# The order of small matmuls over the partition groups, and second factors on 128 partitions, in a two-layer RWKV-7 and mLSTM trunk

## The chip, the cores and the metric

The kernel runs on one core of one Trainium2 chip. The metric is the device time of one execution in microseconds (us), from the median of several runs. A core has TensorE (PE in the profile; its weight loads are listed apart as PEld), VectorE (DVE), ScalarE (ACT), GpSimd (POOL) and SyncE (SP), which issues most of the DMAs. The granted clock of TensorE stands in the profile as a share: 1.00 is 2.4 GHz and 0.50 is 1.2 GHz.

## What is computed

The input is a sequence of 1024 frames of 1024 features, and all is fp32. Layer 0 mixes time with RWKV-7, layer 1 with a chunkwise mLSTM, each is followed by a SwiGLU block, and a norm ends it. What the change touches is the following.

```python
w_log = -softplus(-(w0 + tanh(wl) @ w2)) - 0.5          # decay: second factor w2, 64 x 1024
a = sigmoid(a0 + al @ a2)                               # rate: second factor a2, 64 x 1024

def _rwkv7_step(state, inp):                            # per head, 64 x 64 state, frame by frame
    r_t, w_t, k_t, v_t, a_t, b_t = inp
    sa = einsum('bhvk,bhk->bhv', state, a_t)
    state = state * w_t[:, :, None, :] + sa[..., None] * b_t[:, :, None, :] + v_t[..., None] * k_t[:, :, None, :]
    return state, einsum('bhvk,bhk->bhv', state, r_t)

# mLSTM, in chunks: the scores of queries and keys, times a decay mask
w_intra = exp(d_log - m_t[..., None]) * einsum('bhctd,bhcsd->bhcts', q, k)
```

There are 16 RWKV heads of 64 features and 8 mLSTM heads with 64 features for queries and keys.

## The kernel before

The RWKV recurrence is computed in chunks of 64 frames. A chunk needs the inverse of a unit triangular 64 x 64 matrix, which is built from small blocks. The work is cut into 16 tasks: 8 pairs of heads (128 partitions are two heads of 64) by two halves of 512 frames, so that a task holds 8 chunks of two heads each. The method `chunks` runs the tasks as a pipeline. In step i it calls `rw_chain` for task i-3 (the recurrence over the 8 chunks), `rw_solve` for task i-2, `rw_inverse` for task i-1, `rw_prep` for task i and `rw_finish` for task i-3. Between these calls it takes pieces from a list of fillers: the large projections of the second half (values, decay, rate, keys, receptances, gate) and later the output projection. The fillers are matmuls of 128 x 128 weights on 512 columns, of type fp32r.

A scheduling layer puts each engine's instructions into their final order ahead of time, from the program's order, from priorities (`ahead`) and from what it takes to be ready. On the chip each engine then runs its list in that order and waits on semaphores.

PSUM has eight banks under these tags: `dn` twice, and `c1`, `c2`, `px`, `iv`, `sc`, `tr` once each. The profile leaves numbers out of names, so `c1` and `c2` are both `c` there. A tag with one bank is free for its next user when the reader of the last has read it.

An fp32 matmul appears in the trace as two records, each with a weight load; an fp32r matmul is one record. A shape such as `64*128` in a row counts the partitions that the weights span, and the output partitions. A matmul with weights on 64, 32 or 16 partitions uses one part of the array, its tile; the partitions of the operands and of the output set which.

`rw_inverse` (L657): VectorE inverts 16 x 16 diagonal blocks (L675, L677); a trip through DRAM puts them on four partition groups, q = 0 to 3, at partitions 32q. Two products join them to 32 x 32 blocks: 32 matmuls into `iv` (L701), a copy by ScalarE, and 32 more (L709). Then, for e = 0 and e = 1 one after the other (e is the parity of the chunk), two products of 8 matmuls each join these to 64 x 64 (L724 and L728), with a copy by ScalarE behind each (L725 and L729) and a bank `iv` for each. The index c counts the 8 blocks of a parity.

`rw_solve` (L731): values and one operand are transposed; then 16 matmuls into `px` (L758), copied to `Z`, and 16 more into `px` (L765), copied to `VU` by two ScalarE instructions (L767 and L768). Last, for e = 0 and then 1, eight matmuls go into `tr` (L775) and VectorE copies them into `AR` (L776). `rows(c)` gives the partition halves that chunk c uses.

`ml_prep` (L1284): for the two heads h of a pair, four matmuls of 64 x 128 weights on 128 columns make the scores (L1325) in a bank that alternates between `sc` and `iv`, and VectorE multiplies them by the mask (L1326). It runs eight times.

`lora` (L428): decay and rate, for each half of the frames. The first factor's columns stand twice, so that its output has 128 rows in two equal halves. `st` holds the rounded weights (high part) on rows 0 to 63 and the rest (low part) on rows 64 to 127; `th` and `tl` are high and low part of the activations. L448 is one matmul of `st` on `th`, and L449 one of `hi` on `tl`, on 64 partitions. There are 8 column blocks in each of four calls, so 32 such pairs.

Every matmul that `mm` issues has the line L207 in the profile, so tiles tell them apart.

## Time and profile before

| | |
|---|---|
| median of 3 runs | 3062.93 us (3058.17 to 3084.75) |
| profiled execution | 3071.16 us |
| its span | 3069.2 us |
| mean granted clock of TensorE | 0.919 |
| TensorE busy | 2875.5 us, 94% of the span |
| VectorE, ScalarE busy | 2041.1 us, 1409.5 us |
| the pipeline of RWKV tasks | about 220 to 1180 us of the span |
| the mLSTM mixer | about 1840 to 2360 us of the span |

A span is the profiled part of one execution. Matmuls are pipelined: the time of a record holds its way through the array, and what a matmul costs in a stream is the distance from its start to the next one's start. In the rows of the timeline, equal instructions that follow each other are one row, with the start of the first, the time from there to the end of the last, and their count behind the x.

### The profile page before, as it was taken

Reading aid. Unit: us, or ns where it says so; the run is one execution under the profiler, and the core shown is the slowest. Engines: PE = TensorE matmul, PEld = TensorE weight load, DVE = VectorE, ACT = ScalarE, POOL = GpSimd, SP = SyncE. Lnnn points to the kernel's source line nnn. Section 1 sums busy time; section 2 is a strip of 40 time slices with the busy share of each in tenths; the row PEclk is TensorE's granted clock in tenths of the full one; section 3 lists DMA queues with packets and bytes.
Section 4 is the critical chain, followed back from the end, with each engine's and each line's share of the span. In section 5 each row is a group of like instructions: output and inputs, shape, how many; then the busy total and the mean of one; then the engine's idle time right before and its main releaser. Section 6 shows DMA issues by size and latency. Waiting matters only on the chain.

```text
span 3069.2 us, 46769 instructions
## 1 busy us (share of the span) xinstructions
PE 2875.5 (94%) x17080; PEld 2254.1 (73%) x17080; DVE 2041.1 (67%) x4029; ACT 1409.5 (46%) x2641; POOL 73.5 (2%) x98
## 2 busy tenths in 40 slices
PE   6799989999989898999999998999989999999998
PEld 5577657677767677788877776777857788887776
DVE  7866665757666545978887758755555766667645
ACT  5756665656655554532224335322344533332532
POOL 0000000000000000000000000000010000000000
PEclk9899767979979689999999999988989999999999
DMA  8774433435354236466778854344545233336734
GB/s 289 258 236 141 111 98 92 116 101 142 102 155 125 80 95 210 151 191 220 239 243 281 270 178 157 115 124 151 158 134 168 93 117 103 103 114 229 256 120 149
DMA packets 359721, 492.38 MB, mean 160 GB/s; under 512 B 125212, under 2 KB 208796, under 8 KB 359492
## 3 DMA queue, kind: packets, MB, share of 16 engines
q1 hardware_dynamic: 345668, 464.24, 47.9%
q10 hardware_dynamic: 13824, 25.17, 2.2%
q8 instruction: 134, 2.20, 0.3%
q14 instruction: 95, 0.78, 0.1%
HBM read 359.77 MB, written 129.50 MB: 159 GB/s over the span
## 4 chain that ended last, share of the span: by engine, by line
PE 61%; DVE 13%; DMA 12%; issue 7%; ACT 5%; POOL 1%; SPq 1%; DVEq 0%; POOLq 0%; ACTq 0%
PE dn L207 23%; PE c L207 18%; PE iv L207 8%; PE px L207 6%; PE sc L207 4%; DMA tt<-gd 2%; DMA wraw<-in_wdn 2%; DMA wraw<-wsd 1%; DMA bgs<-in_ada 1%; DVE wq L212 1%; ACT wq L211 1%; DVE ga L212 1%; PE tr L207 1%; DMA bgs<-in_wdn 1%; DMA wsd<-bgs 1%
## 5 line engine op out<-in xcount | busy, mean ns | idle before, releaser
L207 PE MATMUL dn<-a,whi 128*128 128x512 f32 (+1 forms) x1224 | 473.2, 451 | 19.1 <-ACT a L211 7.8
L207 PE MATMUL c<-ga,wq 128*128 128x512 f32 x1446 | 355.6, 395 | 10.2 <-ACT ga L211 8.6
L211 ACT ACTIVATE wq<-wraw 128x1024 fp32r<-128x1024 f32 x202 | 210.7, 1057 | 330.9 <-DVE wraw L890 82.0
L207 PEld LDWEIGHTS c<-ga,wq 128*128 128x128 f32 x1446 | 271.9, 190 | 76.2 <-ACT ga L211 11.5
L207 PEld LDWEIGHTS dn<-a,whi 128*128 128x128 f32 (+1 forms) x1224 | 242.8, 206 | 89.4 <-issue 14.6
L212 DVE TENSOR_TENSOR wq<-wraw,wq 128x1024 fp32r<-128x1024 f32 x202 | 244.3, 1221 | 85.1 <-ACT wq L211 84.8
L207 PE MATMUL dn<-a,wlo 128*128 128x512 f32 (+2 forms) x640 | 284.1, 448 | 7.6 <-ACT tmp L420 3.0
L207 PE MATMUL c<-gb,wq 128*128 128x512 f32 x894 | 221.6, 399 | 7.6 <-DVE wq L212 6.9
L207 PEld LDWEIGHTS c<-gb,wq 128*128 128x128 f32 x894 | 169.5, 192 | 47.9 <-DVE wq L212 8.0
L207 PEld LDWEIGHTS dn<-a,wlo 128*128 128x128 f32 (+2 forms) x640 | 131.3, 206 | 40.2 <-issue 6.8
L211 ACT ACTIVATE whi<-wraw 128x1024 fp32r<-128x1024 f32 (+2 forms) x96 | 100.4, 1046 | 127.4 <-PE dn L207 104.1
L212 DVE TENSOR_TENSOR wlo<-wraw,whi 128x1024 fp32r<-128x1024 f32 (+2 forms) x96 | 116.1, 1209 | 48.4 <-ACT whi L211 41.3
L207 PE MATMUL iv<-ga,wq 128*128 128x512 f32 x552 | 136.0, 389 | 0.0
L207 PE MATMUL px<-ga,wq 128*128 128x512 f32 x528 | 128.6, 389 | 0.0
L207 PEld LDWEIGHTS iv<-ga,wq 128*128 128x128 f32 x552 | 103.6, 188 | 21.5
L211 ACT ACTIVATE w<-wraw 128x384 fp32r<-128x384 f32 (+1 forms) x100 | 56.7, 567 | 129.6 <-PE c L207 55.0
L207 PEld LDWEIGHTS px<-ga,wq 128*128 128x128 f32 x528 | 99.1, 188 | 20.7
L207 PE MATMUL dn<-gb,wq 128*128 128x512 f32 x426 | 104.7, 397 | 5.2 <-ACT gb L211 4.7
L207 PE MATMUL iv<-gb,wq 128*128 128x512 f32 x432 | 104.9, 390 | 0.0
L207 PEld LDWEIGHTS dn<-gb,wq 128*128 128x128 f32 x426 | 81.3, 192 | 24.5 <-ACT gb L211 5.6
L207 PEld LDWEIGHTS sc<-AR,KB 64*128 64x128 f32 x512 | 77.9, 226 | 28.5 <-issue 14.0
L207 PE MATMUL sc<-AR,KB 64*128 64x128 f32 x512 | 94.6, 331 | 3.9 <-DVE KB L612 3.2
(600 smaller groups left out, 5761.7 us busy)
## 6 DMA issues: line engine op xcount, KB each, us to landing
wraw<-in_wgu SPq DMA_DIRECT2D x110, 512.0 KB, 3.6
tt<-gd SPq DMA_DIRECT2D x154, 256.0 KB, 4.0
KT<-in_ada SPq DMA_DIRECT2D x40, 512.0 KB, 5.4
gd<-x SPq DMA_DIRECT2D x77, 256.0 KB, 2.1
gd<-tt SPq DMA_DIRECT2D x72, 256.0 KB, 2.2
wraw<-wsd SPq DMA_DIRECT2D x32, 512.0 KB, 4.5
bgs<-in_ada SPq DMA_DIRECT2D x96, 128.0 KB, 3.4
wraw<-in_wdn SPq DMA_DIRECT2D x24, 512.0 KB, 4.4
```

What stands on the lines that cost most here:

```text
L207: return self.nc.tensor.matmul(out, lhsT, rhs, start=start, stop=stop, **kw)
L211: self.nc.scalar.activation(hi, src, AF.Copy)
L212: self.nc.vector.tensor_tensor(lo, src, hi.bitcast(F32), SUB)
```

## The change

Four methods change. In `lora` the second matmul of a pair takes all 128 rows: `st` on `tl`. In `rw_inverse` the loops over q and over c are exchanged, so that neighbouring matmuls belong to different partition groups; the two parities e, which were done one after the other, go into one bank and alternate. In `rw_solve` the matmuls into `px` alternate between the parities one by one instead of by two, and the last products of e = 0 and e = 1 get two banks (`tr` and now `px`), are written in alternation, and are copied behind that. In `ml_prep` the scores of the two heads are written in alternation into `sc` and `iv`.

```diff
             self.mm(ps, st[:, c], th, start=True, stop=False)
-            self.mm(ps, hi[0:64, c], tl[0:64], start=False, stop=True)
+            self.mm(ps, st[:, c], tl, start=False, stop=True)
...
         ps = self.bank("iv", [P, 8, 16])
-        for q in range(4):
-            r, e = slice(32 * q, 32 * q + 16), 0 if q >= 2 else 1
-            o = 32 * (q % 2) + 16
-            for c in range(8):
+        for c in range(8):
+            for q in range(4):
+                r, e = slice(32 * q, 32 * q + 16), 0 if q >= 2 else 1
+                o = 32 * (q % 2) + 16
                 self.mm(ps[r, c, :], SA[r, e, c, o:o + 16], XN[r, c, 0:16], tile_position=(32 * q, 32 * q))
...
         ps = self.bank("iv", [P, 8, 16])
-        for q in range(4):
-            r = slice(32 * q, 32 * q + 16)
-            for c in range(8):
+        for c in range(8):
+            for q in range(4):
+                r = slice(32 * q, 32 * q + 16)
                 self.mm(ps[r, c, :], Y1[r, c, 0:16], XB[r, c, :], tile_position=(32 * q, 32 * q))
...
-        for e in range(2):
-            o = 0 if e else 64
-            r0, r1 = slice(o, o + 32), slice(o + 32, o + 64)
-            ps = self.bank("iv", [P, 8, 32])
-            for c in range(8):
+        ends = [(e, o, slice(o, o + 32), slice(o + 32, o + 64)) for e, o in enumerate((64, 0))]
+        ps = self.bank("iv", [P, 8, 32])
+        for c in range(8):
+            for e, o, r0, r1 in ends:
                 self.mm(ps[r1, c, :], SA[r0, e, c, 32:64], XN[r0, c, :], tile_position=(o, o + 32))
+        for e, o, r0, r1 in ends:
             nc.scalar.activation(Y1[r1], ps[r1], AF.Copy)
-            ps = self.bank("iv", [P, 8, 32])
-            for c in range(8):
+        ps = self.bank("iv", [P, 8, 32])
+        for c in range(8):
+            for e, o, r0, r1 in ends:
                 self.mm(ps[r0, c, :], Y1[r1, c, :], XD[r1, c, :], tile_position=(o + 32, o))
+        for e, o, r0, r1 in ends:
             nc.scalar.activation(SA[r0, e, :, 32:64], ps[r0], AF.Copy)
...
-        for c in range(8):
-            vr, ur = self.rows(c)
-            for h in range(2):
-                o = (c // 2) * P + 64 * h
-                self.mm(ps[ur, o:o + 64], SA[vr, c % 2, 2 * (c // 2) + h, :], VU[vr, c, 64 * h:64 * h + 64])
+        pairs = [(2 * u + e, h, u * P + 64 * h, *self.rows(e)) for u in range(4) for h in range(2) for e in range(2)]
+        for c, h, o, vr, ur in pairs:
+            self.mm(ps[ur, o:o + 64], SA[vr, c % 2, 2 * (c // 2) + h, :], VU[vr, c, 64 * h:64 * h + 64])
...
+        ps = [self.bank(tag, [P, 4, 64]) for tag in ("tr", "px")]
+        for u in range(4):
+            for h in range(2):
+                hs = slice(64 * h, 64 * h + 64)
+                for e in range(2):
+                    ur = self.rows(e)[1]
+                    self.mm(ps[e][hs, u, :], AT[ur, u, hs], SA[ur, e, 2 * u + h, :])
         for e in range(2):
-            ps = self.bank("tr", [P, 4, 64])
-            ur = self.rows(e)[1]
-            for u in range(4):
-                for h in range(2):
-                    hs = slice(64 * h, 64 * h + 64)
-                    self.mm(ps[hs, u, :], AT[ur, u, hs], SA[ur, e, 2 * u + h, :])
-            nc.vector.tensor_copy(AR[:, e::2, ur], ps)
+            nc.vector.tensor_copy(AR[:, e::2, self.rows(e)[1]], ps[e])
...
+        ps = [self.bank(tag) for tag in ("sc", "iv")]
+        for c in range(4):
+            cs = slice(c * P, c * P + P)
+            for h in range(2):
+                hr = slice(64 * h, 64 * h + 64)
+                self.mm(ps[h][:, cs], k[hr, cs], q[hr, cs])
         for h in range(2):
-            hr = slice(64 * h, 64 * h + 64)
-            ps = self.bank(self.alt("sc", "iv"))
-            for c in range(4):
-                cs = slice(c * P, c * P + P)
-                self.mm(ps[:, cs], k[hr, cs], q[hr, cs])
-            nc.vector.scalar_tensor_tensor(dm[h], ps, 0.125, dm[h], MUL, MUL)
+            nc.vector.scalar_tensor_tensor(dm[h], ps[h], 0.125, dm[h], MUL, MUL)
```

The second loop over `pairs`, into the other bank `px` of the solve, changes in the same way. Three places in the final order of TensorE follow, first of before and then of after. Rows name the output, the moving operand and the weights; `x8` is 8 equal matmuls that follow each other, whatever their tile.

The joining of 32 x 32 blocks in one task of the inverse, before: 8 matmuls of one parity are a row, and the third row of `iv` is the other parity's.

```order
L207 MATMUL iv_6252<-XN_6159,SA_5710 32x32 x8
L207 MATMUL dn_6644<-a_5801,whi_6640 128x512
L207 MATMUL dn_6644<-a_5800,wlo_6641 128x512
L207 MATMUL dn_6644<-a_5807,whi_6640 128x512
L207 MATMUL dn_6644<-a_5808,whi_6640 128x512
L207 MATMUL iv_6262<-XD_6161,Y_1149_6251 32x32 x8
L207 MATMUL c_1198_6492<-st_1582,AR_5146 128x128
L207 MATMUL dn_6644<-a_5807,wlo_6641 128x512
L207 MATMUL dn_6644<-a_5814,whi_6640 128x512
L207 MATMUL iv_6272<-XN_6159,SA_5710 32x32 x8
```

The same task after, on TensorE:

```order
L207 MATMUL iv_6238<-XN_6145,SA_5696 32x32 x16
L741 MATMUL tr_6549<-kc,ld_6546 128x128 x2
L207 MATMUL dn_6837<-a_5758,wlo_6834 128x512
L207 MATMUL dn_6837<-a_5765,whi_6833 128x512
L207 MATMUL c_302_1589<-VU_5993,KT_5191 64x64 x2
L207 MATMUL c_1184_6494<-VU_5993,SR_5146 64x64
L207 MATMUL iv_6257<-XD_6147,Y_1135_6237 32x32 x16
```

Four groups of 8 became two groups of 16, in which the parities alternate; this holds for all 16 tasks. The groups of 32 matmuls of 16 x 16, two for each task, stay whole, and within them the tile now changes from one matmul to the next.

The end of the solve of one task, before; `px` with `Z` is the second product, `tr` with `AT` the last ones of the two parities.

```order
L207 MATMUL iv_10419<-XN_10306,SA_9919 32x32 x8
L207 MATMUL px_10742<-Z_10723,SA_9919 64x64 x2
L207 MATMUL tr_10761<-SA_9919,AT_10715 64x64 x8
L207 MATMUL dn_10880<-a_10866,whi_10875 128x512
L207 MATMUL iv_10429<-XD_10308,Y_1830_10398 32x32 x8
L207 MATMUL dn_10880<-a_10865,wlo_10876 128x512
L207 MATMUL dn_10880<-a_10869,whi_10875 128x512
L207 MATMUL dn_10880<-a_10870,whi_10875 128x512
L207 MATMUL dn_10880<-a_10869,wlo_10876 128x512
L207 MATMUL px_10742<-Z_10723,SA_9919 64x64 x14
L207 MATMUL tr_10771<-SA_9919,AT_10715 64x64 x8
```

The same end after, on TensorE:

```order
L207 MATMUL px_10712<-Z_10693,SA_9891 64x64
L207 MATMUL tr_10731<-SA_9891,AT_10685 64x64
L207 MATMUL px_10712<-Z_10693,SA_9891 64x64 x15
L207 MATMUL tr_10731<-SA_9891,AT_10685 64x64 x7
L207 MATMUL dn_10850<-a_10836,whi_10845 128x512
L207 MATMUL dn_10850<-a_10835,wlo_10846 128x512
L207 MATMUL dn_10850<-a_10839,whi_10845 128x512
L207 MATMUL dn_10850<-a_10840,whi_10845 128x512
L207 MATMUL px_10732<-SA_9891,AT_10685 64x64 x8
```

The last products of the two parities still stand as two groups of 8; the second of them is in `px` now, behind the product of `Z` in that bank, in all 16 tasks.

The scores of one call of `ml_prep` (`iv` and `sc` with two tiles `x`), before:

```order
L207 MATMUL iv_18347<-x_17411,x_17467 128x128 x4
L207 MATMUL dn_18379<-a_17330,whi_18374 128x512
L207 MATMUL dn_18379<-a_17329,wlo_18375 128x512
L207 MATMUL dn_18379<-a_17336,whi_18374 128x512
L207 MATMUL dn_18379<-a_17337,whi_18374 128x512
L207 MATMUL tr_18070<-kc,st_17961 128x1 x2
L207 MATMUL dn_18379<-a_17336,wlo_18375 128x512
L207 MATMUL sc_18353<-x_17411,x_17467 128x128 x4
```

The same call after, on TensorE:

```order
L207 MATMUL iv_18316<-x_17379,x_17435 128x128 x4
L207 MATMUL dn_18347<-a_17298,whi_18342 128x512
L207 MATMUL dn_18347<-a_17297,wlo_18343 128x512
L207 MATMUL dn_18347<-a_17304,whi_18342 128x512
L207 MATMUL dn_18347<-a_17305,whi_18342 128x512
L207 MATMUL tr_18038<-kc,st_17929 128x1 x2
L207 MATMUL dn_18347<-a_17304,wlo_18343 128x512
L207 MATMUL sc_18315<-x_17379,x_17435 128x128 x4
```

Nothing moved but the head that stands first: the four matmuls of each head are still one group, in all eight calls. Over the whole program the tile size of TensorE changes 832 times in the order of after, and 924 times in that of before.

## Rows read from the trace of the kernel before

**Rows 1.** A stretch from:to; its length, busy us of each engine, granted clock, DMA, GB/s.
```profile
220.00:1180.00 960.00, 906.30 (x8176) 668.35 (x8176) 589.32 (x1492) 564.78 (x1315) 31.90 (x32) 0.82 0.41 118
```

**Rows 2.** Stretches at half clock in the pipeline, 18 in all: first, one, last, sum.
```profile
277.10:280.50 3.40, 3.40 (x25) 2.11 (x22) 0.89 (x3) 2.73 (x8) 0.00 (x0) 0.50 0.92 280
...
440.90:475.00 34.10, 32.98 (x282) 24.19 (x278) 15.44 (x48) 18.49 (x40) 0.00 (x0) 0.50 0.23 69
...
1099.70:1120.20 20.50, 20.50 (x173) 15.35 (x169) 6.23 (x13) 8.48 (x20) 0.00 (x0) 0.50 0.20 65
sum 331.00, PE 315.67 PEld 229.36 DVE 159.56 ACT 168.40 POOL 9.14; mean PE 17.54 PEld 12.74 DVE 8.86 ACT 9.36 POOL 0.51
```

**Rows 3.** Timeline of TensorE ahead of the second of these: start, us, instruction.
```profile
437.55 1.52 PE L207 MATMUL iv<-XN,SA 16*16 16x16 f32 x64
439.00 0.33 PE L818 MATMUL tr<-kc,Ys 128*128 128x128 f32 x1
...
440.27 1.59 PE L207 MATMUL iv<-XB,Y 16*16 16x16 f32 x64
```

**Rows 4.** Timeline, the first 12 records (one tile) of such a group alone.
```profile
622.10 0.46 PE L207 MATMUL iv<-XN,SA 16*16 16x16 f32 x12
```

**Rows 5.** Timeline of TensorE, 32 x 32 groups at full clock and at half.
```profile
722.29 0.39 PE L207 MATMUL dn<-a,whi 128*128 128x512 f32 x1
722.52 0.40 PE L207 MATMUL dn<-a,wlo 128*128 128x512 f32 x1
722.84 0.69 PE L207 MATMUL iv<-XN,SA 32*32 32x32 f32 x16
723.46 0.50 PE L207 MATMUL dn<-a,whi 128*128 128x512 f32 x1
...
445.40 1.06 PE L207 MATMUL iv<-XN,SA 32*32 32x32 f32 x16
446.39 0.47 PE L739 MATMUL tr<-kc,ld 128*128 128x128 f32 x1
```

**Rows 6.** Tile `iv` with min/median/max ns; groups with busy us, mean ns.
```profile
L207 PE MATMUL iv<-XD,Y x512: 191/236/258, 281.6 to 1114.0; 32*32 32x32 f32 x171
...
L207 PE MATMUL iv<-XN,SA 32*32 32x32 f32 x512 | 30.1, 223 | 2.0 <-DVE X L677 1.2 <-DVE XN L713 0.8
```

**Rows 7.** Timeline, scores of two heads that follow each other directly.
```profile
2005.16 1.40 PE L207 MATMUL sc<-x,x 64*128 64x128 f32 x5 [0.89 <-DVE pt L1306]
2006.19 0.55 PE L207 MATMUL iv<-x,x 64*128 64x128 f32 x1
```

**Rows 8.** Timeline of TensorE in `lora`, full clock and then half.
```profile
160.17 0.39 PE L207 MATMUL c<-a,wlo 128*128 128x512 f32 x1
160.49 0.50 PE L207 MATMUL c<-a,whi 64*128 64x512 f32 x1
160.92 0.49 PE L207 MATMUL c<-a,wlo 128*128 128x512 f32 x1
161.34 0.50 PE L207 MATMUL c<-a,whi 64*128 64x512 f32 x1
...
401.34 0.79 PE L207 MATMUL dn<-a,wlo 128*128 128x512 f32 x1
402.06 0.79 PE L207 MATMUL dn<-a,whi 64*128 64x512 f32 x1
```

**Rows 9.** Timeline of TensorE, two fillers next to each other at half clock.
```profile
473.34 0.63 PE L207 MATMUL dn<-a,wlo 128*128 128x512 f32 x1
473.77 1.05 PE L207 MATMUL dn<-a,whi 128*128 128x512 f32 x2
```

**Rows 10.** Timeline of TensorE and ScalarE, the end of one task's solve.
```profile
857.05 1.20 PE L207 MATMUL px<-Z,SA 64*64 64x64 f32 x32
860.26 0.71 PE L207 MATMUL tr<-SA,AT 64*64 64x64 f32 x16 [1.96 <-DVE AR L776]
...
858.28 0.59 ACT L767 ACTIVATE VU<-px 64x512 f32<-64x512 f32 x1 [0.44 <-PE px L207]
```

More of the change, by code (lines that the diff above doesn't have):

```diff
@@ L753, in rw_solve @@
         ps = self.bank("px")
-        for c in range(8):
-            vr, ur = self.rows(c)
-            for h in range(2):
-                o = (c // 2) * P + 64 * h
-                self.mm(ps[ur, o:o + 64], SA[vr, c % 2, 2 * (c // 2) + h, :], VU[vr, c, 64 * h:64 * h + 64])
+        pairs = [(2 * u + e, h, u * P + 64 * h, *self.rows(e)) for u in range(4) for h in range(2) for e in range(2)]
+        for c, h, o, vr, ur in pairs:
+            self.mm(ps[ur, o:o + 64], SA[vr, c % 2, 2 * (c // 2) + h, :], VU[vr, c, 64 * h:64 * h + 64])
         nc.scalar.activation(Z, ps.rearrange("p (u f) -> p u f", f=P), AF.Copy)
         ps = self.bank("px")
-        for c in range(8):
-            vr, ur = self.rows(c)
-            for h in range(2):
-                o = (c // 2) * P + 64 * h
-                self.mm(ps[ur, o:o + 64], SA[ur, c % 2, 2 * (c // 2) + h, :], Z[ur, c // 2, 64 * h:64 * h + 64])
+        for c, h, o, vr, ur in pairs:
+            self.mm(ps[ur, o:o + 64], SA[ur, c % 2, 2 * (c // 2) + h, :], Z[ur, c // 2, 64 * h:64 * h + 64])
         p3 = ps.rearrange("p (u f) -> p u f", f=P)
@@ L768, in rw_solve @@
         nc.scalar.activation(VU[0:64, 1::2, :], p3[0:64], AF.Copy)
-        for e in range(2):
-            ps = self.bank("tr", [P, 4, 64])
-            ur = self.rows(e)[1]
-            for u in range(4):
-                for h in range(2):
-                    hs = slice(64 * h, 64 * h + 64)
-                    self.mm(ps[hs, u, :], AT[ur, u, hs], SA[ur, e, 2 * u + h, :])
-            nc.vector.tensor_copy(AR[:, e::2, ur], ps)
+        ps = [self.bank(tag, [P, 4, 64]) for tag in ("tr", "px")]
[5 more added lines that the diff above has]
+                    self.mm(ps[e][hs, u, :], AT[ur, u, hs], SA[ur, e, 2 * u + h, :])
+        for e in range(2):
+            nc.vector.tensor_copy(AR[:, e::2, self.rows(e)[1]], ps[e])
         S["VU"] = VU
```

## The prediction

> **What bounds the kernel now.** The stretches come first. The pipeline of RWKV tasks holds TensorE busy 906.3 of 960.0 us, VectorE 589.3 and ScalarE 564.8 [rows 1]. So the pipeline is paced by TensorE, and a microsecond that its stream loses is worth at most 906.3 / 960.0 = 0.94 us at the end, while the other engines have a third of their time to spare. The granted clock there is 0.82, and the stretches at half clock say why: 18 of them, 331.0 us together, with TensorE busy in 315.7 [rows 2]. TensorE is what everything waits for at half clock too.
>
> The timeline ahead of the second of the shown stretches is the next view. Two groups of 64 records of 16 x 16 run between 437.55 and 441.9, and the clock falls to 1.2 GHz at 440.9 [rows 2, 3]. Eleven of the 18, 198 us together by their lengths, begin like this, during or right behind a task's groups of 16 x 16; the first and the last shown are two of them. The reader is to see that these small groups cost twice: by their own length, and by what the clock does behind them.
>
> Third, how closely the records stand. The first tile's 12 records take 0.46 us [rows 4]; with 0.19 us for a single record (the least that one of 32 x 32 takes, [rows 6]) the distance from start to start is (0.46 - 0.19) / 11 = 25 ns. A whole group is 1.45 us from its start to the next instruction's [rows 3], though four tiles of 16 records one after the other would be 1.60: a tile's first records already run beside the last of the tile ahead. The two heads' scores show the same: with 8 records of `sc` ahead of 8 of `iv`, `iv` begins at 2006.19, when five of `sc` have begun [rows 7]. So two tiles do run side by side, but a record only gets ahead of some three that wait for their own tile; a block of 16 or 8 records keeps the other tiles out.
>
> **The 16 x 16 groups.** There are 32 of them (two in each of 16 tasks), with four tiles of which the next now stands two records away. I take it that two tiles run at any time, as in the rows: 32 steps of 25 ns are 0.80 us, and leaving the group costs 0.12 (1.45 less 1.52 - 0.19), so 0.92 against 1.45. 32 x 0.53 = 17 us. The ends: nothing more than now (0), and four at a time (16 steps, 0.52 us: 30 us). I stay with two, since no row has three.
>
> **The 32 x 32 groups.** Now 64 groups of 16 records in one tile each. To the next instruction such a group takes 0.62 us at full clock and 0.99 at half [rows 5]. A record takes 191 ns at the one and 236 at the other, the mean is 223 [rows 6], so (223 - 191) / 45 = 0.71 of them, 45 groups, run at half clock: 45 x 0.99 + 19 x 0.62 = 56 us. The order of after has 32 groups of twice the length with two tiles alternating. If the two run side by side, each takes what a single one does now, and half of the 56 goes: 28 us. Entering a group costs 0.32 - 0.23 = 0.09 us over two fillers' distance [rows 5], and 32 are gone: 3 us. The ends: if the tiles don't overlap, only 32 times entering and leaving, 0.09 + 0.12, are saved (7 us); 31 is the other end and my value, because both tiles lie in different partition groups as those of the 16 x 16 do. ScalarE's copies (two behind each group) are the same in number.
>
> **The second factors.** A matmul on 64 partitions between such on 128 has 0.43 us behind it and 0.32 to 0.42 ahead of it at full clock [rows 8], where fillers stand 0.23 apart [rows 5]: 0.39 us too much. At half clock it is 0.72 on either side against 0.43 [rows 8, 9]: 0.58. On 128 partitions the tile stays as it is and both go. 32 of them are 12 us at full clock and 19 at half; some stand next to each other and share a side, so I take 13. The weights and activations that it reads exist already, and no copy is added.
>
> **The solve.** The products into `px` alternate by one instead of by two. 32 records take 1.20 us, some 32 ns each, and run among records of the next product already [rows 10]; I take 0, between a loss of 1 and a gain of 3. The last products don't alternate in the order of after: the groups of the two parities stand apart. What changes is what the second waits for. It now follows `Z`'s product in `px`, so it waits for both of ScalarE's copies (0.59 us each, [rows 10]) in place of VectorE's copy of the first. In the shown task that copy made TensorE wait 1.96 us, to 860.26, while ScalarE's two ended at 859.5: there it would gain 0.8. In the order shown four fillers stand between, which hide 4 x 0.23 = 0.92 of the 1.18. I take a loss of 0.27 for each of 16 tasks, 4 us, between a gain of 13 and a loss of 19 (nothing hidden). Queued behind the waiting matmul are fillers and the recurrence of the task ahead.
>
> **The scores.** The order of after has the same groups of four in all eight calls, so this part does nothing to the time: 0.
>
> **The sum.** 17 + 28 + 3 + 13 + 0 - 4 + 0 = 57 us of TensorE's stream. Not all of it arrives: where the stream gets shorter, TensorE reaches waits on VectorE and ScalarE sooner. Between 0.94 and 0.6 (the share that VectorE has of the stretch, [rows 1]) I take 0.8: 46 us.
>
> The clock comes on top. With the inverse shorter, fillers fill more of the time behind which the clock falls. What takes 1 us at half clock takes 0.23 / 0.43 = 0.53 us at full for a filler and 0.62 / 0.99 = 0.63 for a 32 x 32 group, so a microsecond that is granted the full clock gives back about 0.4. If a third of the 198 us goes, that is 66 x 0.4 x 0.8 = 21 us; the ends are 0 and the whole 198 (79 us).
>
> Together 67 us: the profiled execution, 3071 us with its span of 3069, becomes 3004. The median of the runs is 8 us below it, so I predict 3063 - 67 = 2996 us.
>
> **Rivals.** (a) More of it: three or four tiles run at once (30 us for 17) and two thirds of those stretches at half clock go. (57 + 13) x 0.9 + 132 x 0.4 = 116: 2947 us; with all of the 198, some 2920. For it: the distance of 25 ns is a tile's own, since the next tile's first record is not held by it. Against it: nothing in the trace has more than two at once. By the Trainium skill, "TensorE: Matmul & The Clock Gate", section "Part 3: Packing small matmuls — row/col tiling", concurrent tiles start some 4 ns apart; by that the 16 x 16 groups would go to the 30 us end.
>
> (b) The saved time turns into waits. The order is fixed, and behind the inverse stand VectorE's and ScalarE's steps and the DMAs of the next task; if only a third of the 57 us arrives, 20 us, and the clock gives nothing, it is 3063 - 20 = 3043. For it: at 860.26 TensorE waits 1.96 us for VectorE [rows 10]. Against it: TensorE is busy 95% even of the stretches at half clock (315.7 / 331.0).
>
> (c) Tiles that write into one bank take turns. The alternating tiles of the inverse share the bank `iv`; were they kept apart, the inverse would save 7 us only: (7 + 13 - 4) x 0.8 = 13, 3050 us. Against it: in [rows 3, 4] 64 records of four tiles in that one bank take less than four tiles in turn. The Trainium skill, "TensorEngine Tiling (Array Packing)", section "Restrictions and Gotchas", has this rule: different row tiles cannot access the same PSUM bank at a time, so that they would need banks of their own. The trace does not agree with it.
>
> (d) Slower: the bank `px`. The last product of the solve now sits in `px` until VectorE has copied it, and the next task's preparation needs that bank; VectorE's copy stands in its queue behind what waits for DMAs. TensorE runs its list in order, so fillers wait too. A wait as long as the shown one is 1.96 us; this decides once TensorE waits (67 + 31) / 16 = 6.1 us more in each task, some three such waits. That gives 3063 + 31 = 3094 us and above. Against it: preparation stands some way behind the solve in the program, and the copy takes 0.4 us.
>
> **How the numbers follow.** The forecast has 0.58, (a) 0.15, (b) 0.17, (c) 0.05, (d) 0.05. The likeliest is the forecast: 2996 us. The range goes from 2940 (most of (a)) to 3043 (the middle of (b)); outside lie half of (b), (c), (d) and the end of (a), less than 2 in 10. A measurement of this kernel can tell about 1%, 31 us, from no change: faster means below 3032, slower above 3094. Faster: the forecast, (a) and a quarter of (b), 0.77; the same: the rest of (b) and (c), 0.18; slower: (d), 0.05.
>
> **What would show it.** A 16 x 16 group about 0.9 us from its start to the next instruction's (0.5 in (a), 1.4 in (c)); a 32 x 32 group with 32 records and still 0.6 us at full clock (1.1 in (c)); matmuls of the second factor 0.23 us apart; the granted clock of the pipeline above 0.82, with fewer than 11 falls behind the 16 x 16 groups, and the scores as before. In (d) TensorE's waits for VectorE's copies into `AR` or for the `px` users of the preparation grow to microseconds in each task. The prediction is wrong if the pipeline's TensorE time falls by the 57 us and its length does not, or if the clock falls as often as before although the groups got shorter.

## The result, and the profile after

The changed kernel takes 2974.22 us (median of four runs, 2972.92 to 2984.36) where the kernel before takes 3064.2 us beside it (four runs, one more than in the table ahead, 3058.17 to 3084.75): a ratio of 0.970, with a 95% interval of 0.966 to 0.974. The forecast was 2996 us with a range of 2940 to 3043. Direction and range hold; the gain of 90 us is a third larger than the 67 that were worked out.

All of it arises up to the end of the pipeline of RWKV tasks. Measured from the first 16 x 16 group to the last matmul of the recurrence, the pipeline of before is this line of a view by stretches (length, busy us of PE, PEld, DVE, ACT and POOL with counts, granted clock, DMA share, GB/s):

```profile
273.20:1148.50 875.30, 829.02 (x7803) 609.67 (x7802) 535.65 (x1380) 517.32 (x1225) 30.04 (x29) 0.81 0.39 112
```

The same stretch of after, between the same two instructions:

```profile
269.30:1047.60 778.30, 718.12 (x7795) 524.95 (x7794) 533.40 (x1379) 513.77 (x1223) 32.00 (x29) 0.88 0.44 126
```

It begins 3.9 us earlier and is 97.0 us shorter, 100.9 together; 3.2 us are given back later, so that the span ends 97.7 us earlier (2971.5 against 3069.2). TensorE is busy 110.9 us less, and idle for 778.3 - 718.1 = 60.2 us where it was 875.3 - 829.0 = 46.3. VectorE and ScalarE do the same work in less time. The clock went from 0.81 to 0.88. The stretches at half clock, which were 18 with 331.0 us [rows 2], are now 12 (again first, some, last, sum):

```profile
276.20:289.85 13.65, 12.28 (x119) 9.40 (x120) 9.99 (x32) 9.34 (x16) 0.00 (x0) 0.50 0.41 131
...
361.50:392.20 30.70, 28.32 (x328) 18.43 (x328) 19.52 (x54) 24.58 (x44) 0.00 (x0) 0.50 0.29 81
...
945.20:986.15 40.95, 35.15 (x377) 26.19 (x375) 24.64 (x59) 24.16 (x56) 1.92 (x1) 0.50 0.32 83
sum 191.04, PE 174.34 PEld 130.29 DVE 123.01 ACT 119.56 POOL 10.76; mean PE 14.53 PEld 10.86 DVE 10.25 ACT 9.96 POOL 0.90
```

Next, the timeline of TensorE after, at the places of [rows 3, 5, 7, 8, 10]: start, length from the first start to the last end, instruction.

```profile
160.08 0.62 PE L207 MATMUL dn<-a,wlo 128*128 128x512 f32 x2
160.54 0.62 PE L207 MATMUL c<-a,wlo 128*128 128x512 f32 x2
161.00 0.95 PE L207 MATMUL sc<-kc,mt 128*128 128x1 f32 x8
...
395.56 0.69 PE L207 MATMUL iv<-XN,SA 16*16 16x16 f32 x64
396.18 0.73 PE L207 MATMUL dn<-a,wlo 128*128 128x512 f32 x2
...
402.93 1.06 PE L207 MATMUL iv<-XD,Y 32*32 32x32 f32 x32
403.93 0.79 PE L207 MATMUL sc<-AR,KB 64*128 64x128 f32 x2
...
621.25 0.69 PE L207 MATMUL iv<-XN,SA 32*32 32x32 f32 x32
621.87 0.44 PE L741 MATMUL tr<-kc,ld 128*128 128x128 f32 x2
...
830.28 0.68 PE L207 MATMUL px<-SA,AT 64*64 64x64 f32 x16
830.89 0.27 PE L207 MATMUL c<-VU,KT 128*64 128x64 f32 x1
...
1908.50 1.40 PE L207 MATMUL sc<-x,x 64*128 64x128 f32 x5 [0.88 <-DVE pt L1304]
1909.53 0.55 PE L207 MATMUL iv<-x,x 64*128 64x128 f32 x1
```

A group of 64 records of 16 x 16 is 396.18 - 395.56 = 0.62 us from its start to the next instruction's, against 1.45 [rows 3]. A group of 32 records of 32 x 32 takes 0.62 at full clock and 1.00 at half, as long as one of 16 records did [rows 5]. A pair of a second factor is the distance of 0.46 us, so 0.23 for each matmul. The last product in `px` is 0.61 us with 16 records. The scores begin just as in [rows 7]: `iv` 1.03 us behind `sc`, when five of `sc` have begun. From the starts of all 128 score records, they take 20.3 us in either kernel.

What does the engine do before the clock falls? First three stretches of 7 us (a length chosen for the view) that end where a stretch at half clock begins, in the kernel before:

```profile
655.80:662.80 7.00, 7.00 (x155) 5.78 (x154) 2.92 (x9) 2.02 (x8) 0.00 (x0) 1.00 0.73 243
758.20:765.20 7.00, 6.99 (x157) 5.92 (x156) 3.10 (x8) 1.49 (x6) 0.00 (x0) 1.00 0.66 190
986.90:993.90 7.00, 6.94 (x161) 5.54 (x159) 1.70 (x6) 3.92 (x10) 0.00 (x0) 1.00 0.80 193
```

And three in the kernel after:

```profile
320.40:327.40 7.00, 3.29 (x25) 1.91 (x25) 6.88 (x18) 6.99 (x11) 0.00 (x0) 1.00 0.14 37
542.30:549.30 7.00, 5.80 (x27) 4.05 (x25) 6.90 (x26) 1.79 (x5) 0.00 (x0) 1.00 0.34 102
938.20:945.20 7.00, 4.81 (x42) 3.83 (x42) 5.67 (x18) 5.37 (x13) 1.64 (x1) 1.00 0.46 139
```

In before, TensorE was busy all the time, and 128 of the some 155 records are of 16 x 16. In after it ran 25 to 42 records, of larger matmuls, and waited for 1.2 to 3.7 us. Over all falls: in before, nine of the 18 came with less than 0.2 us of idle time ahead of them, all nine behind 16 x 16 groups; in after, each of the 12 has at least 0.99 us of idle time in such a stretch, and the three that also have a 16 x 16 group in it are no exception. So in this execution the falls behind small groups without a wait are gone, and those behind waits are left. That the waits bring these falls is not tested, and the traces of single parts, below, show that it isn't the alternation of the small groups alone that takes the others away. The waits of TensorE after, in the pipeline (engine, line, releaser: us in total, times, longest):

```profile
PE sc L207 <- DVE KB L612: 6.9, 3, 4.0
PE c L207 <- DVE VU L786: 5.2, 9, 1.0
...
PE iv L207 <- ACT Y L725: 3.7, 5, 1.1
...
PE iv L207 <- ACT Y L704: 2.4, 6, 1.0
...
PE c L207 <- DVE AR L774: 1.9, 3, 0.9
...
PE px L207 <- DVE AR L774: 0.2, 1, 0.2
```

And in before:

```profile
PE tr L207 <- DVE AR L776: 3.7, 3, 2.0
...
PE sc L207 <- DVE KB L612: 3.2, 1, 3.2
...
PE iv L207 <- ACT Y L725: 1.4, 2, 1.0
...
PE iv L207 <- ACT Y L704: 0.7, 1, 0.7
```

Those that grew stand where the saved time ran out: for `KB` 6.9 us, where it was 3.2, and for ScalarE's copies between the inverse's products (`Y`, 3.7 and 2.4 us, where they were 1.4 and 0.7). The wait of the last products for VectorE's copy out of `tr` (1.96 us in [rows 10], 3.7 us over the pipeline) is gone, and that for `px` is 0.2 us in all; but products of the recurrence (`c`) now wait 1.9 us for the copies into `AR`, for which they had no wait in before.

### The profile page after: what moved, and what is told of

Its sections match the earlier page's. It is cut to its first block, busy times and chain, and to the rows that moved or that the text cites. A ratio compares the mean times of both kernels' runs of the same rounds, so it can differ in the third digit from the quotient of the medians.

```text
span 2971.5 us, 46769 instructions
## 1 busy us (share of the span) xinstructions
PE 2766.4 (93%) x17080; PEld 2176.9 (73%) x17080; DVE 2039.4 (69%) x4029; ACT 1405.6 (47%) x2641; POOL 74.4 (3%) x98
## 4 chain that ended last, share of the span: by engine, by line
PE 55%; DVE 15%; DMA 14%; issue 7%; ACT 6%; SPq 2%; POOL 1%; DVEq 0%; POOLq 0%; ACTq 0%
PE dn L207 20%; PE c L207 17%; PE iv L207 6%; PE px L207 6%; PE sc L207 4%; DMA bgs<-in_ada 2%; DMA wraw<-in_wdn 2%; DMA wraw<-wsd 2%; DVE wq L212 1%; DMA tt<-gd 1%; ACT wq L211 1%; DMA bgs<-in_wdn 1%; DMA wsd<-bgs 1%; DMA KT<-in_ada 1%; DMA st<-in_ada 1%
## 5 line engine op out<-in xcount | busy, mean ns | idle before, releaser
L207 PE MATMUL dn<-a,whi 128*128 128x512 f32 (+1 forms) x1200 | 441.2, 433 | 17.4 <-ACT a L211 6.4
L207 PEld LDWEIGHTS dn<-a,whi 128*128 128x128 f32 (+1 forms) x1200 | 229.6, 198 | 79.2 <-ACT a L211 8.8
L207 PE MATMUL dn<-a,wlo 128*128 128x512 f32 (+1 forms) x664 | 281.5, 436 | 1.3 <-DVE wlo L477 0.6
L207 PEld LDWEIGHTS dn<-a,wlo 128*128 128x128 f32 (+1 forms) x664 | 132.5, 202 | 32.9 <-issue 4.2
L211 ACT ACTIVATE w<-wraw 128x384 fp32r<-128x384 f32 (+1 forms) x100 | 56.7, 567 | 131.8 <-PE c L207 58.4
```

The lines of the kernel that those rows point to most:

```text
L207: return self.nc.tensor.matmul(out, lhsT, rhs, start=start, stop=stop, **kw)
L211: self.nc.scalar.activation(hi, src, AF.Copy)
```

## The experiments

Each kernel was timed in five rounds beside the kernel before, whose median was 3069.8, 3069.4 and 3069.8 us in the three sets. The mean granted clock over all runs of the kernel before is 0.919 (33 runs, 0.910 to 0.927); clocks below are such means over a kernel's runs. "Stream" is what TensorE needs from a group's start to the next instruction's, at the clock that it had and with any wait in between. A trace is one execution, and from one execution of the kernel before to another the mean clock differs by up to 0.017, so a sum of half clock or a count of falls in one trace is less sure than a mean clock over runs.

### One part of the change at a time

**The second factors alone** (`lora`):

```diff
-            self.mm(ps, hi[0:64, c], tl[0:64], start=False, stop=True)
+            self.mm(ps, st[:, c], tl, start=False, stop=True)
```

> Only the second factors of decay and rate on 128 partitions; all else as before. Both theories: 32 matmuls cheaper by 0.39 us at full and 0.58 at half clock, 13 us less stream, of which 5 us by the end of the first half's share (about 200 us of the span), 8 more in the pipeline; time 3051 (3046 to 3058). The half-clock stretches of the pipeline stay near 331 us.

Measured: 3042.77 us, ratio 0.990 (0.988 to 0.992), clock 0.924. The pipeline begins 5.5 us earlier (267.7), 0.34 for each of the 16 matmuls ahead of it, as expected; but the whole gain is 27 us, not 13, and the time lies under the stated range. Half clock in the pipeline, which was to stay, went from 331 to 304 us in the trace, and 27 x 0.4 = 11 us make up most of the difference.

**The 16 x 16 products alone:**

```diff
-        for q in range(4):
...
-            for c in range(8):
+        for c in range(8):
+            for q in range(4):
```

> Only the loops over q and c exchanged in the two 16 x 16 products. My theory now (the clock hangs on the 16 x 16 groups): each group 0.62 us to the next instruction instead of 1.45, 25 us of the stream, and nearly all of the 132 us of half clock that the changed kernel lost go here: 25 x 0.9 + 132 x 0.4 = 75 us, 2988. Rival 1 (the clock follows whatever makes TensorE's groups short, each part by its share): 25 x 0.9 + 50 x 0.4 = 42 us, 3021. Rival 2 (the clock follows from the shorter 32 x 32 groups and the solve): 23 us, 3040, and half clock stays near 331 us.

Measured: 3029.59 us, ratio 0.986 (0.984 to 0.989), clock 0.929. The groups take 0.62 us as in the whole change. My theory (2988) fell, and so did rival 2 (3040); rival 1 is nearest, with 40 us against its 42. The pipeline's line:

```profile
270.90:1099.20 828.30, 773.32 (x7803) 561.86 (x7802) 535.35 (x1380) 515.70 (x1225) 30.02 (x29) 0.85 0.41 118
```

TensorE idles 828.3 - 773.3 = 55.0 us, 8.7 more than before. Half clock in the pipeline is 253 us, 79 less than before, in 16 falls. One of them still comes behind 16 x 16 groups without a wait, although they alternate; 119 of the 151 records of the 7 us ahead of it are theirs:

```profile
515.87:522.87 7.00, 7.00 (x151) 5.10 (x151) 4.91 (x12) 4.02 (x9) 0.00 (x0) 1.00 0.80 250
```

**The 32 x 32 products alone** (both parities in one bank, in alternation):

```diff
-        for e in range(2):
...
-            ps = self.bank("iv", [P, 8, 32])
-            for c in range(8):
+        ps = self.bank("iv", [P, 8, 32])
+        for c in range(8):
+            for e, o, r0, r1 in ends:
                 self.mm(ps[r1, c, :], SA[r0, e, c, 32:64], XN[r0, c, :], tile_position=(o, o + 32))
```

> Only the 32 x 32 products: both parities in one bank, alternating. My theory now (the clock hangs on the 16 x 16 groups): 28 us of the stream, 25 of them at the end, 3038, and the half clock stays near 331 us. Rival 1 (the clock follows every shorter group): 25 + 55 x 0.4 = 47 us, 3016. Rival 2 (the clock follows from here and the solve): 25 + 132 x 0.4 = 78 us, 2985.

Measured: 3009.17 us, ratio 0.980 (0.977 to 0.982), clock 0.937. My theory (3038, half clock near 331 us) fell: the gain of 61 us lies between those of rival 1 (47) and rival 2 (78). This part alone lifts the clock nearly as far as the whole change (0.938), though it leaves every 16 x 16 group as long as it was at either clock. In its trace half clock in the pipeline is 208 us in 13 falls, and of these only two come behind 16 x 16 groups with less than 0.2 us of idle time ahead, where before has nine: a change elsewhere took most such falls away too. The pipeline's line:

```profile
275.90:1082.50 806.60, 751.33 (x7806) 554.32 (x7805) 531.86 (x1380) 517.57 (x1227) 32.38 (x29) 0.87 0.43 121
```

**The solve and the scores alone:**

```diff
+        for c, h, o, vr, ur in pairs:
...
-            ps = self.bank("tr", [P, 4, 64])
+        ps = [self.bank(tag, [P, 4, 64]) for tag in ("tr", "px")]
...
-            ps = self.bank(self.alt("sc", "iv"))
+        ps = [self.bank(tag) for tag in ("sc", "iv")]
```

> Only the solve (its products into px by one, its last products into tr and px) and the scores. My theory: 5 us of TensorE's stream, given back by waits, so within 8 us of before, 3063; the mLSTM part no different at all. Rival: the second bank px frees TensorE from its waits for VectorE's copies into AR (3.7 us in the pipeline before) and brings part of the clock: 3040. The other rival, that px is held too long: 3075 and more, with waits of TensorE for the copies into AR or by the preparation's users of px.

Measured: 3049.44 us, ratio 0.992 (0.989 to 0.995), clock 0.922. No loss through `px`: TensorE idles less (40.0 us), and of the waits around the last products 0.9 us for ScalarE's `VU` and 0.5 us for `AT` are left, with 0.7 us of the recurrence's products for the copies into `AR`. The scores take the same 20.3 us, so the gain is the solve's. My theory (within 8 us) fell; in size, 20 us, the gain is the first rival's (23), and what it named is there: the wait of the last products for VectorE's copies into `AR` (3.7 us) is gone, and half clock in the pipeline is 27 us less. That the one brought the other is not shown. The kernel with the second factors alone, whose solve is as before, has 27 us less of half clock too, and of that wait it has only this:

```profile
PE tr L207 <- DVE AR L776: 0.5, 1, 0.5
```

By ratios the four parts gain 1.0, 1.4, 2.0 and 0.8%, 5.2% together, and the whole change gains 3.0%. The lifts of the clock add up to 0.034, and that of the whole change is 0.019. The missing 2.2% are some 68 us. The clock's share is estimated from this: 0.015 x 2 x 3000 = 90 us of half clock, some 36 us at 0.4 each; 5 us are idle time (the parts alone add 8.4 us to it, the whole change 13.9). The other 27 are not accounted for; each ratio has an interval of some 0.3% to either side, 9 us.

### One part undone or varied, and two more places

**The changed kernel without the 16 x 16 part:**

```diff
-        for c in range(8):
-            for q in range(4):
+        for q in range(4):
...
+            for c in range(8):
```

> The changed kernel, with only the 16 x 16 products in their old loop order. Theory A (the parts share one stock of half clock: with the 32 x 32 groups changed it is all but gone): 25 us of stream come back, x 0.9 = 22, 2996, and the pipeline's half clock stays near 200 us. Theory B (each part brings its own): the 79 us of half clock that this part took when alone come back too, 22 + 79 x 0.4 = 54, 3028.

Measured: 3008.0 us, ratio 0.978 (0.974 to 0.982), clock 0.931. It lies between the theories, in time and in half clock (239 us in the pipeline, between 200 and 270): the clock falls by 0.007, nearly as much as this part had lifted it alone (0.009).

**The 32 x 32 products merged, but in turn:**

```diff
-        for c in range(8):
-            for e, o, r0, r1 in ends:
+        for e, o, r0, r1 in ends:
+            for c in range(8):
                 self.mm(ps[r1, c, :], SA[r0, e, c, 32:64], XN[r0, c, :], tile_position=(o, o + 32))
```

The second product likewise.

> The changed kernel, with the 32 x 32 products of both parities still merged into one bank, but eight of one parity and then eight of the other. Theory A (two tiles side by side): a group of 32 records takes some 1.1 us instead of 0.62, 32 x 0.5 = 16 us at full clock, 25 at half; with a part of the half clock back: 3000 (2990 to 3035). Theory B (the merging brings it: half as many groups, ScalarE's copies behind each other): 2978, and the half clock as in the changed kernel.

Measured: 2987.23 us, ratio 0.972 (0.969 to 0.975), clock 0.937. The timeline of this kernel:

```profile
632.19 1.09 PE L207 MATMUL iv<-XN,SA 32*32 32x32 f32 x32
633.21 0.44 PE L741 MATMUL tr<-kc,ld 128*128 128x128 f32 x2
```

1.02 us against 0.62 with alternation, for the same 32 records between the same instructions: this is theory A's direct part. Over all groups the stream is 16 us longer. The clock did not fall. The time itself lies between theory B's 2978 and the 2990 at which theory A's range begins, and is not told apart from the changed kernel's (the intervals of the ratios overlap); the trace tells it.

**The preparation's products alternate too:**

```diff
-            for h in range(2):
-                hs = slice(64 * h, 64 * h + 64)
-                ps = self.bank("sc", [P, 4, P])
-                for q in range(4):
-                    self.mm(ps[:, q], KB[hs, 4 * u + q, :], AR[hs, 4 * u + q, :])
+            two = [self.bank(tag, [P, 4, P]) for tag in ("sc", "px")]
+            for q in range(4):
+                for h in range(2):
+                    hs = slice(64 * h, 64 * h + 64)
+                    self.mm(two[h][:, q], KB[hs, 4 * u + q, :], AR[hs, 4 * u + q, :])
+            for h, ps in enumerate(two):
```

> The changed kernel, and one more place treated in the same way: the products of the preparation (KB with AR, 64 x 128, four of one head and then four of the other, each pair of records some 0.27 us) alternate between the two heads' partition halves, into the banks sc and px. Theory A (side by side as the others): 512 records at half their distance, 512 x 0.11 / 2 = 28 us of stream, 0.8 of it: 2952, with more if the clock follows. Theory B (TensorE's list is fuller now and px, which three methods share, gets waits): no gain, 2974 to 2990, with TensorE's idle time in the pipeline above 60 us.

Measured: 2934.02 us, ratio 0.954 (0.951 to 0.957), clock 0.945: better than the changed kernel. First one head's eight records in the timeline of the changed kernel:

```profile
296.13 1.16 PE L207 MATMUL sc<-AR,KB 64*128 64x128 f32 x8
297.22 0.49 PE L207 MATMUL c<-st,AR 128*128 128x128 f32 x2
```

In that of this kernel the heads stand side by side:

```profile
240.05 0.37 PE L207 MATMUL sc<-AR,KB 64*128 64x128 f32 x1
240.06 0.37 PE L207 MATMUL px<-AR,KB 64*128 64x128 f32 x1
240.26 0.27 PE L207 MATMUL sc<-AR,KB 64*128 64x128 f32 x1
240.27 0.27 PE L207 MATMUL px<-AR,KB 64*128 64x128 f32 x1
...
241.14 0.73 PE L207 MATMUL dn<-a,whi 128*128 128x512 f32 x2
```

Sixteen records of both heads take 241.14 - 240.05 = 1.09 us, as long as eight of one head did (297.22 - 296.13). All 512 fell from 88.1 us to 55.4. Theory B's waits are there as well (idle time 69.5 us against 60.2), but cost less than the stream gave.

**The solve's last products alternate** in the final order, too, with `iv` in place of `px`:

```diff
-        ps = [self.bank(tag, [P, 4, 64]) for tag in ("tr", "px")]
+        ps = [self.bank(tag, [P, 4, 64]) for tag in ("tr", "iv")]
```

> The changed kernel, with the last products of the solve in tr and iv instead of tr and px; in the final order the two parities alternate there. Theory A: one group of 32 records with four tiles instead of two groups of 16 with two: 16 tasks x (0.46 + 0.15) us less = 9 us, 2966. Theory B (the bank iv, which the next task's inverse needs four times, is held, or the tr group now waits for what the second needed): 2985 and more, with TensorE's waits for the copies into AR or by iv.

Measured: 2954.96 us, ratio 0.961 (0.957 to 0.964), clock 0.946. Its timeline shows four records at a time:

```profile
533.44 0.27 PE L207 MATMUL tr<-SA,AT 64*64 64x64 f32 x1
533.45 0.27 PE L207 MATMUL iv<-SA,AT 64*64 64x64 f32 x1
533.46 0.27 PE L207 MATMUL tr<-SA,AT 64*64 64x64 f32 x1
533.46 0.27 PE L207 MATMUL iv<-SA,AT 64*64 64x64 f32 x1
533.55 0.22 PE L207 MATMUL tr<-SA,AT 64*64 64x64 f32 x1
```

The last products' stream went from 26.5 to 18.0 us, which is theory A's size (9). That the time fell by about twice as much goes with the clock (0.938 to 0.946), although idle time rose to 73.9 us.

### Which half of the 32 x 32 part, and both additions

**Only the merging, on the kernel before:**

```diff
-        for e in range(2):
...
-            ps = self.bank("iv", [P, 8, 32])
+        ps = self.bank("iv", [P, 8, 32])
+        for e, o, r0, r1 in ends:
             for c in range(8):
```

> The kernel before, with only the merging of the 32 x 32 groups: both parities in one bank, eight of one and then eight of the other, so that half as many groups stand in the order and no two tiles alternate. Theory M (half as many groups with their waits for ScalarE: this is what brought the clock when the 32 x 32 part was alone): 60 us less the 13 of the alternation, 3022, mean clock 0.93 or more. Theory S (the tiles side by side brought the clock): only the 7 us of entering and leaving 32 groups fewer, 3060, mean clock 0.92.

Measured: 3030.95 us, ratio 0.988 (0.985 to 0.991), clock 0.930. Between the theories, nearer to M in time and clock. With the alternation on top it was 3009 us and 0.937.

**The two additions together:**

```diff
+            two = [self.bank(tag, [P, 4, P]) for tag in ("sc", "px")]
...
+        ps = [self.bank(tag, [P, 4, 64]) for tag in ("tr", "iv")]
```

> The changed kernel, with the products of the preparation alternating between the heads (banks sc and px) and the last products of the solve between the parities (banks tr and iv), both at once. If their gains of 40 and 19 us add up: 2915. If they share the half clock that is left, as the parts of the change did: 2925. If the banks px, tr and iv are held too long now: 2934 and more, with TensorE's idle time in the pipeline above 75 us.

Measured: 2922.07 us, ratio 0.952 (0.950 to 0.955), clock 0.947. The fastest kernel of the study; its interval overlaps that of the preparation alone. Against the changed kernel's ratio it gains 1.8%, where the two alone gained 1.6 and 1.0, which speaks for a shared stock. The traces agree: half clock in the pipeline is 191 us in the changed kernel, 140 and 150 with one addition each, and 133 with both. TensorE's idle time there is 75.0 us, so waits grew as well.

**Alternating in halves, so with four groups for a task again:**

```diff
+        for g in (slice(0, 4), slice(4, 8)):
+            ps = self.bank("iv", [P, 8, 32])
+            for c in range(g.start, g.stop):
+                for e, o, r0, r1 in ends:
```

The copies follow for each half.

> The changed kernel, with the 32 x 32 products alternating between the parities as there, but in halves: blocks 0 to 3 of both parities first, then blocks 4 to 7, each in a bank of its own with ScalarE's copies behind it (eight in place of four for a task). So there are four groups for a task again, of 16 records each, side by side. Theory M (the number of groups and of their waits counts): the clock falls to that of the changed kernel without this part, 3000 us and more. Theory S (side by side counts): 32 enterings more at 0.21 us, 7 us, 2981, the mean clock still 0.938.

Measured: 2972.12 us, ratio 0.968 (0.965 to 0.971), clock 0.939. Twice as many groups and copies cost nothing that can be measured in the time; in the trace the stream of these groups is 36.0 us against 30.3. Theory M, taken as the sole cause, falls.

**The changed kernel without the 32 x 32 part:**

```diff
-        for c in range(8):
-            for e, o, r0, r1 in ends:
+        for e in range(2):
...
+            for c in range(8):
```

> The changed kernel with the 32 x 32 products as before (one parity behind the other, four groups for a task). Both theories: 28 us of stream come back, x 0.9 = 25. Theory A (the other parts hold the clock without it): 3000, mean clock 0.938. Theory B (this part holds the clock): the clock of the kernel with the other parts, about 0.928 as when the 16 x 16 part was alone, 2 x 0.01 x 3000 = 60 us more at half clock, x 0.4 = 24 more: 3023.

Measured: 3005.93 us, ratio 0.980 (0.977 to 0.983), clock 0.934. Theory A's time, and a clock between the two.

The four kernels that differ only in the 32 x 32 part then read: neither merged nor alternating 3006 us and 0.934, merged 2987 and 0.937, alternating in halves 2972 and 0.939, both 2974 and 0.938. On the kernel before, the same part lifted the clock by 0.017, and its merging alone by 0.011. Neither half of it carries the clock by itself; what a part brings there depends on what else has been changed.

## Why the prediction was right, and where its sizes were off

**What bounds it.** Right: TensorE paced the pipeline, and what its stream lost arrived for the most part. The clock moved with it, as foreseen.

**The 16 x 16 groups.** Predicted 0.92 us and 17 us together, measured 0.62; from the starts of all 32 groups, 47.6 us became 22.4, so 25 us. The step that failed is "I take it that two tiles run at any time": the rows showed two only because a block of 16 records kept the third tile out. Two tiles' worth of stream would have been 0.92; with four in alternation a record follows on average 9.7 ns behind the last (0.62 / 64), with leaving the group counted in. By the Trainium skill, "TensorE: Matmul & The Clock Gate", section "Part 3: Packing small matmuls — row/col tiling", concurrent tiles start some 4 ns apart; the trace is nearer to that than to the 25 ns of a single tile [rows 4]. The four-tile end of the forecast, 0.52 us and 30 us, was the nearer one.

**The 32 x 32 groups.** Right: 32 records in 0.62 us at full clock. From the starts of all groups 58.4 us became 30.3, 28 us against 28 + 3. The kernel with turns shows that it is the alternation: 1.02 us without it. A little of the 28 is the clock's, though: 690 of the 1024 records ran at half clock in before (the forecast had taken 0.71 of them) and 320 in after.

**The second factors.** Right in the stream (0.23 us each, 5.5 us for the first 16, so 0.34 for each). The 0.39 of the forecast took the upper end of the distances of [rows 8], 0.43 + 0.42 - 2 x 0.23; the lower end gives 0.29. The other 16, in the pipeline, were not measured apart.

**The solve.** Predicted a loss of 4 us, measured a gain: its last products took 31.1 us of stream before and 26.5 after, its products into `px` 48.9 and 46.8, 7 us together, and the wait of the last products for VectorE's copy is gone. How much of this is the change's own is open: these streams hold clock and waits, and with the solve as before, the kernel with the 32 x 32 part alone has 25.4 and 42.4 us. The step that failed is the 1.18 us that the second group was to wait for ScalarE's two copies. In the task of the timeline above, ScalarE's second copy ends at 829.41 + 0.60 = 830.01, and the second group starts at 830.28, behind fillers that ran meanwhile:

```profile
828.79 0.59 ACT L764 ACTIVATE VU<-px 64x512 f32<-64x512 f32 x1
829.41 0.60 ACT L765 ACTIVATE VU<-px 64x512 f32<-64x512 f32 x1
```

In the whole pipeline of after no product in `px` waits for these copies.

**The scores.** Right: no change.

**How much arrives.** The stream lost 25 + 28 + 13 + 7 = 73 us (13 for the second factors as predicted), TensorE's idle time grew by 60.2 - 46.3 = 13.9, so by this account 0.81 of it arrived; 0.8 had been taken, between 0.94 and 0.6, and that it fits so closely is partly luck. Rival (b) named the right mechanism, waits at `KB` and at ScalarE's copies in the inverse, and far too large a price.

**The clock.** The term that was mis-sized most. Predicted that 66 us at half clock would go, worth 21 us; 140 went (331 to 191), and at the same worth, 140 x 0.4 x 0.8, that is 45 us. Then 59 + 45 = 104 us, against the 100.9 measured up to the pipeline's end. This split is an estimate. Another comes from busy time alone: TensorE was busy at half clock for 315.7 us [rows 2] and then for 174.3, and 141 x 0.4 = 57 of the 110.9 us of busy time that went are the clock's, 54 the stream's, with 13.9 us lost to waits. In both the clock brought two to three times the 21 us. The forecast took a third of the 11 falls behind 16 x 16 groups; in after no fall comes behind small groups without a wait. By single parts the step was wrong in another way too: it tied the clock to the 16 x 16 groups, while of the single parts the 32 x 32 one lifts the clock most (0.937) and leaves those groups as they are; in its trace such falls are two instead of nine, and with the 16 x 16 part alone there is still one.

**The rivals.** (a) was right on the tiles and on the clock (two thirds of the 198 us, 132, against 140 that went), and too large by 27 us. Some 12 of these are that it let 0.9 of the stream and all of the clock's gain arrive (116 us against the 104 above); the rest lies between the 104 and the 90 us by which the medians differ. (c) is refuted: four tiles that write into the one bank `iv` run side by side, 64 records in 0.62 us. The rule of the Trainium skill, "TensorEngine Tiling (Array Packing)", section "Restrictions and Gotchas", that different row tiles cannot access one bank at a time, doesn't hold in this form: here they write to different partitions of the bank. (Different row tiles that write the same partitions of one bank were not tried.) (d) is refuted: TensorE waits 0.2 us for the `px` users behind that copy, and 1.9 us at the recurrence for copies into `AR`, in all 16 tasks together.

**What stays open.** Why the parts together gain 68 us less than their sum is accounted for, by estimate, for some 41 us (clock and idle time), not for the rest. Why the 32 x 32 part alone lifts the clock more than the 16 x 16 part, though both shorten the stream about equally, isn't settled; that a fall is taken away by one part and would not have come with another is a reading that is argued, and shown only by clocks that don't add up. No run puts in a wait or takes one out by itself, so what makes the clock fall, small groups or waits, is told by what stood ahead of the falls and not by a test.

## What to carry to other kernels

Write small matmuls so that neighbouring ones use different partition groups, and look in the final order whether they still do: products that the scheduler had pulled apart gained another 19 us by the medians once they got a pair of banks that let them alternate, and the next place of the same kind, found by its tile size in the list of costly groups, gained 40. Where a TensorE-bound stage loses its clock, price a change twice, by the stream that it shortens and by the half clock that goes with it; the second was about half of the gain here, by estimate (45 of 104 us, or 57 of 110.9). Gains of several such parts need not add up (5.2% as single parts and 3.0% together here), so time them together.

## What the runs showed of the hardware that was not expected

- Four tiles of 16 x 16 run side by side in one bank, each on its own partitions: 64 records in 0.62 us, 9.7 ns each, against 25 ns within one tile.
- Two tiles of 64 x 128 that share all output partitions, but not the bank, run side by side at full rate: 16 records in 1.09 us, where 8 of one tile took 1.09 us too (at full clock).
- Four tiles of 64 x 64, two parities by two heads, in two banks: four records start within 0.02 us.
- The clock fell behind stretches in which TensorE waited for 1.2 to 3.7 of 7.00 us, and also behind 16 x 16 groups in which it was busy for 7.00 of 7.00 us: there, being busy did not keep it up.
